# An encoder block on one core: a fifth tile of weight halves, two step orders changed, four stores moved

## The chip, the cores and the metric

The kernel runs on one core of one Trainium2 chip. The metric is device time in microseconds (us), the median of the runs; a lower time is better. One execution was also taken with the hardware profiler, and all rows below come from it.

## What is computed

The reference is one layer of an encoder over 256 tokens of width 2048, in float32:

```python
h = rms_norm(x, g_mix)
qa, ka, va, qb, kb, vb, qc, gt = split(h @ w_in)           # 4096 columns, then 3 x 2048 of gates
oa = dilated_windows(qa, ka, va)                           # 6 heads in 3 groups
ob = grouped_queries(rope(qb), rope(kb), vb)               # 6 heads, 2 of keys
oc = cross_attention(qc, rms_norm(mem, g_mem) @ w_mem_kv)  # 4 heads
merged = sigmoid(gt0)*(oa@w_br_a) + sigmoid(gt1)*(ob@w_br_b) + sigmoid(gt2)*(oc@w_br_c)
x = x + merged @ w_o
hf = rms_norm(x, g_ffn) @ w_ffn_in                         # 2 x 5632 columns
x = x + (silu(hf[:, :5632]) * hf[:, 5632:]) @ w_ffn_out
```

Nearly all of the time goes to the products with the weights, some 273 MB that are read once from HBM.

## The kernel before

**Halves.** A weight tile `raw` is 128 rows by 2 x 512 columns of float32 (512 KB), in one of 6 buffers. It enters TensorE as two tiles in a rounded format: `whi`, the rounded weight (ScalarE, line 358 in `halves`, line 123 in the older `product`), and `wlo`, the rest (VectorE, lines 359 and 124). The activations are held as two halves as well, so each product takes three matmuls. There are 4 buffers each of `whi` and `wlo`.

**Stages.** `beginning` (the memory keys) runs through `run` and `pair`. The qkv blocks and the first gates run through `product`, with the attention as side jobs. Then `heads`, a group of pools for what only attention needs (`s2`, 32 KB a partition), is given up, and `run(everything())` does the rest: `merging` (gates and branches), `projecting` (the product with `w_o`, in two pairs of column blocks, n = 0 and n = 2) and `feeding` (11 pairs of `w_ffn`; after 4, 8 and 11 of them two pairs of `w_ffn_out`).

**Steps.** `pair` computes two column blocks c = 0 and c = 1 for 256 tokens by a list of steps. `d3` and `D3` are the plain product of row tile 3 with block 0 or 1: one `raw`, one pair of halves, 12 matmuls. `f3 g3 h3` with a share of `p` and `q` do the same row tile for both blocks by seven multiplications in place of eight: 21 matmuls for 24, but 3.5 pairs of halves for 2, and four more additions on VectorE (lines 449 to 451 in `g`, 465 in `h`). "Light" below means `d` and `D`; "heavy" means `f g h`. The lists are `STEPS...` in lines 53 to 58. `STEPS_O` serves both pairs of `w_o`, `STEPS_FFN` only the first pair of `w_ffn` (line 828).

**Order.** `run` (line 505) has each step make its halves first (`ready`) and do its matmuls later: `AHEAD` = 3 steps wait in between, so four pairs of halves are in flight. TensorE's instructions and the loads on SyncE's queue stay in the order of the program; the halves of all steps stay in order on ScalarE and on VectorE (`nc.follow`). All the rest is placed by a scheduler at build time, with some at high priority. After each step's matmuls `tick` advances one side job. A job that yields n goes on n ticks later.

**What follows a pair.** When the last step of block c is done, `sums` adds up its banks and `done` uses them. For a pair of `w_o` that is `add`: x is updated (line 779), and two ticks later `transposed` (line 266) turns the new columns, in two halves, into `x1T`, through `tp`, a bank of PSUM that ScalarE and VectorE read in turn, twice each (lines 126 and 127 in `split`). With blocks c = 0 and c = 1 that makes four banks, on four successive ticks: first half of block 0, first half of block 1, second half of block 0, second half of block 1. They stand behind the first four steps of the next pair. Then, after n = 0, `sums_of` builds the `forms`, the sums of tokens that `g`, `p` and `q` of `w_ffn` need.

**Banks.** PSUM's eight banks are two groups of four. The accumulators X, Y and Z of a pair and the first halves of `transposed` share the group `at`; V, Q, W and the second halves share `mm` (lines 272 and 386). Y and V are taken by the first `d`, Z and Q by the first `D`, X by the first `f`, W by the first `g`; they stay taken through the pair.

**Stores.** In the last part of `w_ffn_out` the result is stored by SyncE straight behind its sum (line 847), in the same queue as the loads.

Of the kernel before, what the change touches and what calls it, by code (L numbers as in the profile page):

```python
# [11 lines left out]
F32 = mybir.dt.float32  # L12
F32R = mybir.dt.float32r
# [5 lines left out]
P = 128  # L19
S = 256  # L20
T = S // P
D = 2048
KT = D // P
HD = 128
DFF = 5632
NC = 512
KF = DFF // P
PK = 2
# [23 lines left out]

STEPS = "d0 f1 D0 g1 d4 h1 f2 D4 g2 d5 h2 f3 D5 g3 d6 h3 p0 p2 D6 q0 q2 d7 D7".split()
STEPS_GATE = "d0 D0 d4 D4 f1 d5 g1 D5 h1 f2 g2 d6 h2 f3 g3 h3 p0 p2 D6 q0 q2 d7 D7".split()
STEPS_FFN = "d0 D0 f1 d4 g1 D4 h1 f2 d5 g2 D5 h2 f3 d6 g3 h3 p0 p2 D6 q0 q2 d7 D7".split()
STEPS_O = "d0 D0 d1 D1 f2 d4 g2 D4 h2 d5 f3 D5 g3 d6 h3 p0 D6 q0 d7 D7".split()
STEPS_OUT = "d0 D0 d1 D1 d2 D2 f6 d3 g6 D3 h6 f7 d4 g7 h7 p0 D4 q0 d5 D5".split()
STEPS_OUT2 = "d0 f5 D0 g5 d1 h5 f6 D1 g6 d2 h6 f7 D2 g7 d3 h7 p0 p2 D3 q0 q2 d4 D4".split()
AHEAD = 3


class InOrder:
# [37 lines left out]
def encoder_block(ctx: ExitStack, tc: tile.TileContext, a: dict, out: bass.AP):  # L100
    nc = InOrder(tc)
    const = ctx.enter_context(tc.tile_pool(name="const", bufs=1))
    wp = ctx.enter_context(tc.tile_pool(name="wp", bufs=3))
    big = ctx.enter_context(tc.tile_pool(name="big", bufs=11))
    mid = ctx.enter_context(tc.tile_pool(name="mid", bufs=5))
    small = ctx.enter_context(tc.tile_pool(name="small", bufs=4))
    dram = ctx.enter_context(tc.tile_pool(name="dram", bufs=1, space=bass.MemoryType.DRAM))
    psum = ctx.enter_context(tc.tile_pool(name="psum", bufs=4, space=bass.MemoryType.PSUM))

    def s8(shape, name, dt=F32R, pool=None):  # L110
        return (pool or big).tile(shape, dt, name=name, tag="s8")
# [59 lines left out]
    def start(steps):  # L171

        job = [0, steps]
        side.append(job)
        advance(job)
# [55 lines left out]
    def load_T(src, g, tag):  # L231


        tiles = [s8([P, 4, 2, S], tag) for _ in range(KT // 4)]
        raws, have = {}, set()

        def get(k, fetch=False):
            k0 = k // 2 * 2
            tl = tiles[k // 4]
            if k0 not in raws:  # L240
                raws[k0] = wp.tile([P, 2, S], F32, name="rawT", bufs=2)
                nc.sync.dma_start(out=raws[k0], in_=src[k0 // 2].rearrange("p (k s) -> p k s", s=S))
            if not fetch and k0 not in have:
                have.add(k0)
                for i in range(k0, k0 + 2):
                    split(tl[:, i % 4, 0], tl[:, i % 4, 1], raws[k0][:, i - k0], g[:, i:i + 1])
            return tl[:, k % 4, 0], tl[:, k % 4, 1]
        return get
# [46 lines left out]
    two = const.tile([P, 2], F32, name="two")  # L295
    nc.vector.memset(two[:, :1], 1.0)
    nc.scalar.activation(two[:, 1:], two[:, :1], AF.Copy)
    gh = const.tile([P, 6, HD], F32, name="gh")
    rope = const.tile([P, 2, T, HD // 2], F32, name="rope")
    relb = const.tile([P, A_HEADS], F32, name="relb")  # L300

    def constants():
# [7 lines left out]
    def hold(n, steps):  # L310
        yield n
        yield from steps

    def fetch(get, pace):
        for k in range(0, KT, 2):
            get(k)
            yield pace
# [29 lines left out]
            yield 1  # L347


    def halves(*srcs):  # L350

        hi = wp.tile([P, PK, NC], F32R, name="whi", bufs=4)
        lo = wp.tile([P, PK, NC], F32R, name="wlo", bufs=4)
        n = 0
        for v in srcs:
            v = v.unsqueeze(1) if len(v.shape) == 2 else v
            o = slice(n, n + v.shape[1])
            nc.follow(nc.scalar.activation(hi[:, o], v, AF.Copy))  # L358
            nc.follow(nc.vector.tensor_sub(lo[:, o], v, hi[:, o].bitcast(F32)))  # L359
            n += v.shape[1]  # L360
        return hi, lo
# [140 lines left out]
                    done(c, sums(c))  # L502
            yield ending

    def run(pairs):

        nc.on = True
        waiting = []
        for p in pairs:
            for products in p:  # L510
                waiting.append(products)
                if len(waiting) > AHEAD:
                    waiting.pop(0)()
                    tick()
        for products in waiting:
            products()
            tick()
        nc.on = False

    whole_k = lambda n: [d + str(u) for u in range(n) for d in "dD"]  # L520
    block_pair = lambda w, n: lambda u, c: w[n + c][u]


    headT, V = {}, {}
    heads = ExitStack()
    s2 = heads.enter_context(tc.tile_pool(name="s2", bufs=16))

    def take_slots(ps, slots, r, name="x", eng=nc.gpsimd):
# [140 lines left out]
    def beginning():  # L669
        start(hold(5, row_sums(a["mem"], r_m, 3, "mem")))  # L670
        start(hold(10, constants()))
        start(hold(5, fetch(xT, 1)))
        yield pair(block_pair(a["w_mem"], 0), memT, whole_k(KT // 2),
                   lambda c, r: start(take_slots(r, MEM_SLOTS[4 * c:4 * c + 4], r_m, "mem", nc.vector)), operand=memT)

    run(beginning())
    oT = [s8([P, 4, 2, S], f"oT{i}") for i in range(3)]
    ol = lambda k: (oT[k // 4][:, k % 4, 0], oT[k // 4][:, k % 4, 1])
    for c in range(8):
# [16 lines left out]
    finish()  # L696
    heads.close()
    tail = ctx.enter_context(tc.tile_pool(name="tail", bufs=4))
    mT, x1T, x = [], [], []
    ss1 = const.tile([P, T, 4], F32, name="ss1")  # L700

# [66 lines left out]
    def projecting():  # L768
        x.extend(s8([P, D], f"x{t}", F32) for t in range(T))
        for t in range(T):  # L770
            nc.sync.dma_start(out=x[t], in_=a["x"][t * P:(t + 1) * P, :])
        x1T.extend(s8([P, 2, 4, S], "x1T") for _ in range(4))
        mTl = lambda k: (mT[k // 4][:, 0, k % 4], mT[k // 4][:, 1, k % 4])
        oforms = sums_of(mTl, (2, 3), form_room(2))
        for n in (0, 2):
            def add(c, r, n=n):
                xc = [x[t][:, (n + c) * NC:(n + c + 1) * NC] for t in range(T)]
                for t in range(T):
                    nc.vector.tensor_add(xc[t], r[:, t], xc[t])

                def later():
                    yield 1
                    sq = s4([P, T, NC], "sq")
                    for t in range(T):
                        nc.scalar.activation(sq[:, t], xc[t], AF.Square, accum_out=ss1[:, t, n + c:n + c + 1])
                    yield 2
                    yield from transposed(xc, lambda k, m: (x1T[n + c][:, 0, k], x1T[n + c][:, 1, k]),
                                          lambda k: gT[:, 2, 4 * (n + c) + k:4 * (n + c) + k + 1], 2)
                    if n + c == 1:
                        room.extend(form_room(3))  # L790
                        forms.append(sums_of(x1l, (1, 2, 3), room[:3]))
                    elif n + c == 3:
                        yield 2
                        ssr = small.tile([P, T], F32, name="ss", bufs=1)
                        nc.vector.tensor_reduce(ssr, ss1, axis=AX.X, op=ALU.add)
                        row_scale(ssr, r_f)
                start(urgent(later()))
            yield pair(block_pair(a["w_o"], n), mTl, STEPS_O, add, oforms)


    def feeding():
        for c0, c1 in ((0, 4), (4, 8), (8, KF // 4)):
# [4 lines left out]
            for n in range(c0, c1):  # L807
                halves_of = []

                def hidden(c, v, av=halves_of, late=late if n == c1 - 1 else []):  # L810
# [9 lines left out]
                    def later():  # L820
# [6 lines left out]
                    start(urgent(later()))  # L827
                yield pair(lambda u, c, n=n: a["w_ffn"][n][2 * u + c], x1l, STEPS if n else STEPS_FFN, hidden,
                           lambda u, f: forms[0](u, f))
            pairs = whole_k(2 * (c1 - c0)), whole_k(2 * (c1 - c0))  # L830
            out_forms = None
            if not last:
                pairs = STEPS_OUT, STEPS_OUT2
                sums_of(hTl, (5,), room[3:])
                out_forms = by_pair((5, 6, 7), room[3:] + late)
            for n in (0, 2):
                def output(c, r, n=n, last=last):
                    for t in range(T):
                        rt = r[t] if last else r[:, t]
                        for h in range(2 if last and n + c == 3 else 1):  # L840
                            w = NC if not (last and n + c == 3) else NC // 2
                            o = slice((n + c) * NC + h * w, (n + c) * NC + (h + 1) * w)
                            nc.vector.scalar_tensor_tensor(x[t][:, o], rt[:, h * w:(h + 1) * w],
                                                           r_f[:, 0, t:t + 1], x[t][:, o],
                                                           op0=ALU.mult, op1=ALU.add)
                            if last:
                                nc.sync.dma_start(out=out[t * P:(t + 1) * P, o], in_=x[t][:, o])
                yield pair(lambda u, c, n=n, c0=c0: a["w_ffn_out"][n + c][2 * c0 + u], hTl, pairs[n // 2], output,
                           out_forms)

    def everything():
        for stage in (merging, projecting, feeding):
            yield from stage()

    run(everything())
    finish()


# [82 lines left out]
```

## Time and profile before

| | |
|---|---|
| median of 3 runs | 1421.25 us (1418.86 to 1422.56) |
| the profiled execution | 1424.29 us |
| its span, first to last instruction | 1422.5 us |
| TensorE matmul busy | 1392.6 us (98%) |
| VectorE busy | 1125.9 us (79%) |
| ScalarE busy | 804.5 us (57%) |
| mean granted TensorE clock | 0.996 |

The profiled execution spent 1.8 us outside its span. Busy time of a matmul is drawn longer (0.39 us) than the distance at which matmuls follow each other, so a wait of TensorE has to be read from the starts.

### The profile page before, as it was taken

How to read it: one execution, taken by the hardware profiler on the slowest of the kernel's cores; microseconds unless marked ns; L12 is line 12 of the kernel's file. 1: busy time of each engine (PE TensorE's matmuls, PEld its weight loads, DVE VectorE, ACT ScalarE, POOL GpSimd, SP SyncE). 2: the span in 40 equal slices, each digit the busy share in tenths (PEclk: the TensorE clock that was granted, in tenths of full speed). 3: DMA queues.
4: the chain of work that ended last, by engine and by line, in shares of the span. 5: the costliest groups of instructions: out<-in, count | busy, mean ns of one | idle time of the engine just before them, and what ended most of it. 6: DMA issues, size and time to landing. Idle time of an engine off the chain costs nothing.

```text
span 1422.5 us, 17528 instructions
## 1 busy us (share of the span) xinstructions
PE 1392.6 (98%) x6245; PEld 1136.5 (80%) x6245; DVE 1125.9 (79%) x1481; ACT 804.5 (57%) x1096; POOL 76.7 (5%) x146
## 2 busy tenths in 40 slices
PE   8999999999999999999999999999999999999998
PEld 6778878888878888888778888777888877788886
DVE  5767756755788888879988898988889988898844
ACT  6766545644464564656656556555565664466632
POOL 0024533200000000000000000000000000000000
PEclk9999999999999999999999999999999999999999
DMA  8976535556565665756555666566666656556644
GB/s 296 332 237 206 162 112 185 163 163 188 171 205 180 190 223 175 268 171 186 190 172 193 200 192 197 172 220 190 186 201 196 215 171 203 187 183 202 218 129 162
DMA packets 79416, 277.09 MB, mean 195 GB/s; under 512 B 8992, under 2 KB 11552, under 8 KB 79072
## 3 DMA queue, kind: packets, MB, share of 16 engines
q1 hardware_dynamic: 79184, 275.94, 60.7%
q8 instruction: 49, 0.80, 0.2%
q14 instruction: 39, 0.32, 0.1%
q10 hardware_dynamic: 144, 0.02, 0.0%
HBM read 273.05 MB, written 2.88 MB: 194 GB/s over the span
## 4 chain that ended last, share of the span: by engine, by line
PE 75%; DVE 10%; ACT 5%; issue 5%; DMA 2%; POOL 2%; SPq 0%; ACTq 0%; DVEq 0%; POOLq 0%
PE mm L75 17%; PE mmZ L75 12%; PE mmY L75 11%; PE mmV L75 11%; PE mmQ L75 10%; PE mmX L75 7%; DVE wlo L359 5%; ACT whi L358 4%; PE mmW L75 2%; DMA raw<-in_w_mem 1%; DVE raw L450 1%; PE tp L75 1%; DVE t L449 1%; PE sc L75 1%; POOL rot L579 1%
## 5 line engine op out<-in xcount | busy, mean ns | idle before, releaser
L359 DVE TENSOR_TENSOR wlo<-raw,whi 128x1024 fp32r<-128x1024 f32 (+1 forms) x455 | 518.0, 1153 | 154.1 <-ACT whi L358 149.2
L358 ACT ACTIVATE whi<-raw 128x1024 fp32r<-128x1024 f32 (+1 forms) x455 | 444.7, 1001 | 340.8 <-DVE raw L450 74.5
L75 PE MATMUL mm<-whi,xT 128*128 128x512 f32 x768 | 244.5, 395 | 0.0
L124 DVE TENSOR_TENSOR wlo<-raw,whi 128x1024 fp32r<-128x1024 f32 x100 | 128.7, 1296 | 86.1 <-ACT whi L123 85.6
L75 PEld LDWEIGHTS mm<-whi,xT 128*128 128x128 f32 x768 | 144.4, 189 | 29.7 <-issue 0.8
L123 ACT ACTIVATE whi<-raw 128x1024 fp32r<-128x1024 f32 x100 | 105.7, 1071 | 90.6 <-PE mm L75 83.5
L75 PE MATMUL mm<-wlo,xT 128*128 128x512 f32 x384 | 151.3, 394 | 0.0
L75 PE MATMUL mmY<-whi,x1T 128*128 128x512 f32 x286 | 111.3, 390 | 0.0
L75 PE MATMUL mmV<-whi,x1T 128*128 128x512 f32 x286 | 108.6, 392 | 0.0
L75 PE MATMUL mmZ<-whi,x1T 128*128 128x512 f32 x220 | 85.8, 390 | 0.0
L75 PE MATMUL mmQ<-whi,x1T 128*128 128x512 f32 x220 | 85.7, 389 | 0.0
L75 PEld LDWEIGHTS mm<-wlo,xT 128*128 128x128 f32 x384 | 72.7, 189 | 15.7 <-issue 0.8
L75 PE MATMUL mmX<-whi,forms 128*128 128x512 f32 x236 | 79.7, 390 | 0.0
L359 DVE TENSOR_TENSOR wlo<-t,whi 128x1024 fp32r<-128x1024 f32 x76 | 72.2, 982 | 4.8 <-ACT whi L358 4.6
L358 ACT ACTIVATE whi<-t 128x1024 fp32r<-128x1024 f32 x76 | 63.4, 858 | 1.2 <-PE mmX L75 0.7
L75 PEld LDWEIGHTS mmY<-whi,x1T 128*128 128x128 f32 x286 | 53.7, 188 | 11.4
L75 PEld LDWEIGHTS mmV<-whi,x1T 128*128 128x128 f32 x286 | 53.7, 188 | 11.0
L75 PE MATMUL mmY<-whi,hT 128*128 128x512 f32 x156 | 60.4, 391 | 0.0
L75 PE MATMUL mmV<-whi,hT 128*128 128x512 f32 x156 | 60.1, 392 | 0.0
L75 PE MATMUL mmV<-wlo,x1T 128*128 128x512 f32 x143 | 55.8, 390 | 0.0
L75 PE MATMUL mmY<-wlo,x1T 128*128 128x512 f32 x143 | 55.7, 389 | 0.0
L75 PE MATMUL mmZ<-whi,hT 128*128 128x512 f32 x136 | 53.9, 396 | 1.3 <-ACT whi L358 1.3
(258 smaller groups left out, 2711.5 us busy)
## 6 DMA issues: line engine op xcount, KB each, us to landing
raw<-in_w_ffn SPq DMA_DIRECT2D x176, 512.0 KB, 4.2
raw<-in_w_gate SPq DMA_DIRECT2D x96, 512.0 KB, 4.1
raw<-in_w_ffn_out SPq DMA_DIRECT2D x88, 512.0 KB, 4.3
raw<-in_w_qkv SPq DMA_DIRECT2D x64, 512.0 KB, 4.9
raw<-in_w_o SPq DMA_DIRECT2D x32, 512.0 KB, 4.3
raw<-in_w_br SPq DMA_DIRECT2D x24, 512.0 KB, 3.6
raw<-in_w_mem SPq DMA_DIRECT2D x16, 512.0 KB, 6.3
rawT<-in_memT SPq DMA_DIRECT2D x8, 256.0 KB, 4.3
```

Of the source, the lines that this page charges most:

```text
L75: ins = op(*args, **kw)
L123: nc.scalar.activation(hi, src, AF.Copy)
L124: nc.vector.tensor_sub(lo, src, hi.bitcast(F32))
L358: nc.follow(nc.scalar.activation(hi[:, o], v, AF.Copy))
L359: nc.follow(nc.vector.tensor_sub(lo[:, o], v, hi[:, o].bitcast(F32)))
L449: nc.follow(nc.vector.tensor_add(t3[:, those.index(u)], b2[:, 0], b2[:, 1]))
L450: nc.follow(nc.vector.tensor_add(b2[:, 0], b2[:, 0], b1[:, 0]))
L579: op(ov[:, :, :, c], ov[:, :, :, c], tmp[:, :n])
```

## The change

Four things are done together.

1. `gh`, `rope` and `rawT`, 8 KB a partition, move from pools that live to the end into a pool `early`, which is given up together with `heads`. In the room a pool `more` holds one further pair of `whi` and `wlo`: every fifth call of `halves` takes it. `AHEAD` becomes an argument of `run`: 3 for `beginning`, 4 for `everything`.
2. `STEPS_FFN` has two heavy row tiles, not three, and begins with six light steps.
3. The second pair of `w_o` gets a list of its own, `STEPS_O2`: its heavy steps begin with the second step, and its last six are light.
4. A store becomes a side job: for the pair n = 0 it is put four ticks behind its sum, for n = 2 one tick.

```diff
-STEPS_FFN = "d0 D0 f1 d4 g1 D4 h1 f2 d5 g2 D5 h2 f3 d6 g3 h3 p0 p2 D6 q0 q2 d7 D7".split()
+STEPS_FFN = "d0 D0 d1 D1 d4 D4 f2 d5 g2 D5 h2 f3 d6 g3 h3 p0 D6 q0 d7 D7".split()
 STEPS_O = "d0 D0 d1 D1 f2 d4 g2 D4 h2 d5 f3 D5 g3 d6 h3 p0 D6 q0 d7 D7".split()
+STEPS_O2 = "d0 f2 D0 g2 d1 h2 f3 D1 g3 d4 h3 p0 D4 q0 d5 D5 d6 D6 d7 D7".split()
-AHEAD = 3
...
+    heads = ExitStack()
+    early = heads.enter_context(tc.tile_pool(name="early", bufs=1))
...
-                raws[k0] = wp.tile([P, 2, S], F32, name="rawT", bufs=2)
+                raws[k0] = early.tile([P, 2, S], F32, name="rawT", bufs=2)
...
-    gh = const.tile([P, 6, HD], F32, name="gh")
-    rope = const.tile([P, 2, T, HD // 2], F32, name="rope")
+    gh = early.tile([P, 6, HD], F32, name="gh")
+    rope = early.tile([P, 2, T, HD // 2], F32, name="rope")
...
+    count, more = [0], []
+
     def halves(*srcs):
 
-        hi = wp.tile([P, PK, NC], F32R, name="whi", bufs=4)
-        lo = wp.tile([P, PK, NC], F32R, name="wlo", bufs=4)
+        count[0] += 1
+        pool, n = (more[0], 1) if more and count[0] % 5 == 0 else (wp, 4)
+        hi = pool.tile([P, PK, NC], F32R, name="whi", bufs=n)
+        lo = pool.tile([P, PK, NC], F32R, name="wlo", bufs=n)
...
-    def run(pairs):
+    def run(pairs, ahead):
...
-                if len(waiting) > AHEAD:
+                if len(waiting) > ahead:
...
-    run(beginning())
+    run(beginning(), 3)
...
     heads.close()
     tail = ctx.enter_context(tc.tile_pool(name="tail", bufs=4))
+    more.append(ctx.enter_context(tc.tile_pool(name="more", bufs=1)))
...
-            yield pair(block_pair(a["w_o"], n), mTl, STEPS_O, add, oforms)
+            yield pair(block_pair(a["w_o"], n), mTl, STEPS_O2 if n else STEPS_O, add, oforms)
+
+    def store(t, o):
+        nc.sync.dma_start(out=out[t * P:(t + 1) * P, o], in_=x[t][:, o])
+        yield 1
...
-                                nc.sync.dma_start(out=out[t * P:(t + 1) * P, o], in_=x[t][:, o])
+                                start(hold(1 if n else 4, store(t, o)))
...
-    run(everything())
+    run(everything(), 4)
```

## Rows read from the trace of the kernel before

**Rows 1.** The page, part 1: busy us, share of span, instructions of each engine.

```profile
PE 1392.6 (98%) x6245; PEld 1136.5 (80%) x6245; DVE 1125.9 (79%) x1481; ACT 804.5 (57%) x1096; POOL 76.7 (5%) x146
```

**Rows 2.** Waits of PE, whole span: who waited for whom, us, times, longest.

```profile
PE mmW L75 <- DVE wlo L359: 4.2, 11, 0.8
...
PE mmX L75 <- DVE wlo L359: 2.5, 5, 0.5
...
PE mmW L75 <- ACT whi L358: 0.9, 1, 0.9
```

**Rows 3.** Timeline of PE, one `w_ffn` pair: start, us, engine, line, operation, tiles.

```profile
811.63 0.39 PE L75 MATMUL mmQ<-whi,x1T 128*128 128x512 f32 x1
...
812.31 0.39 PE L75 MATMUL mmW<-whi,forms 128*128 128x512 f32 x1
...
813.39 0.39 PE L75 MATMUL mmZ<-whi,forms 128*128 128x512 f32 x1
```

**Rows 4.** Waits of all engines, whole span, same columns as rows 2.

```profile
DVE wlo L359 <- ACT whi L358: 153.8, 207, 4.1
...
ACT whi L358 <- PE mmV L75: 73.4, 51, 2.9
```

**Rows 5.** Timelines of ACT and of DVE; in brackets the idle time before.

```profile
779.58 1.06 ACT L358 ACTIVATE whi<-raw 128x1024 fp32r<-128x1024 f32 x1 [1.17 <-PE mmQ L75]
...
780.68 2.59 DVE L359 TENSOR_TENSOR wlo<-raw,whi 128x1024 fp32r<-128x1024 f32 x2 [0.72 <-ACT whi L358]
...
929.52 0.68 DVE L449 TENSOR_TENSOR t<-raw 128x512 f32<-128x512 f32 x1
...
939.17 0.68 DVE L449 TENSOR_TENSOR t<-raw 128x512 f32<-128x512 f32 x1
```

**Rows 6.** Timeline of PE, first pair of `w_ffn`.

```profile
700.80 0.60 PE L75 MATMUL tp<-ident,x 128*128 128x128 f32 x4
701.65 0.47 PE L75 MATMUL mmX<-whi,x1T 128*128 128x512 f32 x1 [0.25 <-DVE x1T L127]
...
706.31 0.60 PE L75 MATMUL tp<-ident,x 128*128 128x128 f32 x4
709.48 0.77 PE L75 MATMUL mmW<-whi,forms 128*128 128x512 f32 x1 [2.58 <-DVE x1T L127]
...
712.51 0.39 PE L75 MATMUL mmZ<-wlo,x1T 128*128 128x512 f32 x1
```

**Rows 7.** Stretches: length, busy us of PE, PEld, DVE, ACT, POOL; PE clock; DMA.

```profile
650.40:694.60 44.20, 44.20 (x202) 36.23 (x201) 42.07 (x65) 28.91 (x44) 0.00 (x0) 1.00 0.59 188
...
709.40:712.50 3.10, 3.02 (x7) 2.44 (x8) 1.67 (x9) 0.51 (x2) 0.00 (x0) 0.52 0.38 145
```

**Rows 8.** Timelines of PE and DVE: two transposed banks and their last reads.

```profile
653.19 0.60 PE L75 MATMUL tp<-ident,x 128*128 128x128 f32 x4
653.54 0.48 PE L75 MATMUL mmZ<-whi,mT 128*128 128x512 f32 x1
...
659.47 0.87 DVE L127 SCALAR_TENSOR_TENSOR x1T<-tp,gT,x1T 128x256 fp32r<-128x256 f32 x2
...
697.59 0.60 PE L75 MATMUL tp<-ident,x 128*128 128x128 f32 x4
...
701.03 0.47 DVE L127 SCALAR_TENSOR_TENSOR x1T<-tp,gT,x1T 128x256 fp32r<-128x256 f32 x1
```

**Rows 9.** Waits of SP's queue, whole span, same columns as rows 2.

```profile
SPq L75 <- DVE x L843: 40.4, 9, 19.3
```

**Rows 10.** Timelines of PE and ACT near the end.

```profile
1390.66 0.40 PE L75 MATMUL mmV<-whi,hT 128*128 128x512 f32 x1
...
1391.24 1.06 ACT L358 ACTIVATE whi<-raw 128x1024 fp32r<-128x1024 f32 x1 [4.29 <-DMA raw<-in_w_ffn_out]
...
1393.95 0.40 PE L75 MATMUL mmZ<-whi,hT 128*128 128x512 f32 x1
```

More of the change, by code (lines that the diff above doesn't have):

```diff
@@ L524, in encoder_block @@
     headT, V = {}, {}
-    heads = ExitStack()
     s2 = heads.enter_context(tc.tile_pool(name="s2", bufs=16))
```

## The prediction, made before the result was known

> **What bounds the kernel now.** I read the page first. TensorE is busy 98% of the span, VectorE 79%, ScalarE 57% [rows 1]. So the question is how much of TensorE's time is waiting, and the 98% can't say it, because a matmul is drawn 0.39 us long. From the starts the pace is read: from 811.63 to 812.31 three matmuls pass, 0.227 us each [rows 3]. A listed wait of TensorE is therefore 0.16 us longer than its row says (0.39 - 0.23), and one under some 0.3 us is not listed at all.
>
> The view of TensorE's waits comes next [rows 2]. The first product with forms in a `g` step (mmW) waited 11 times for VectorE's `wlo`: 4.2 + 11 x 0.16 = 6.0 us. The chain X in `p` and `q` waited 5 times: 2.5 + 0.8 = 3.3 us. One mmW waited for `whi`: 1.1 us. Not listed is what rows 3 show: the last `g` of a `w_ffn` pair takes 1.08 us from 812.31 to 813.39 for three matmuls, 0.40 us too long. I find this in 8 of the 11 pairs: 3.2 us. That is 13.6 us of small waits for halves, all in heavy stretches.
>
> Then I asked why the halves come late. VectorE waits 154 us in total for `whi`, and ScalarE's `whi` waits 73 us for a mmV, that is for TensorE to give back a buffer [rows 4]. In a light stretch both are held up by the four tiles: ScalarE idles 1.17 us for mmQ, and VectorE behind it 0.72 us [rows 5]. In a heavy stretch VectorE alone is slow: from one `g` to the next it needs 9.65 us (929.52 to 939.17) [rows 5] for steps whose 39 matmuls take 39 x 0.227 = 8.9 us. So the lead is capped when VectorE has time, and eaten up when it has none.
>
> Two larger waits stand alone. At the start of `w_ffn` mmW begins 3.17 us after the last transposition's start, where such a group otherwise delays its successor by 0.35 us [rows 6, 8]; it waited for a read of `tp`, that is for a bank. Near the end 3.29 us pass from 1390.66 to 1393.95 for three matmuls: 2.6 us too long, behind a load that came late [rows 10].
>
> **The change part by part.**
>
> *Stores.* SyncE's queue stood up to 19.3 us at a store that waited for its sum [rows 9], and the loads behind it came too late: the 2.6 us of rows 10. Now the first store of n = 0 stands behind the load of the sixth of the last pair's 12 steps, the others after later loads. By then their sums are long made, so no load waits. Gain 2.6 us. The stores of the last pair remain behind all loads; nothing waits there, and the price is between 0 and 0.4 us (one more short store issue). I take 0.
>
> *The start of `w_ffn`.* Now W is taken by the fifth step, while V, Q and two second halves of `transposed` hold the four banks of `mm`. Wait: 3.17 - 0.35 = 2.8 us. After it the clock was granted at 0.52, the lower level, 1.2 GHz [rows 7]: the seven matmuls from 709.48 to 712.51 took 3.03 instead of 1.59 us, 1.4 us more [rows 6]. X, the third step, had waited as well: 0.85 - 0.35 = 0.5 us. Together 4.7 us. With the new list X comes seventh and W ninth, some 11 us later than now (four light steps of 12 matmuls), when those banks have been read. One heavy row tile becomes plain: 3 more matmuls, 0.7 us. Net gain 4.0 us. If the cover failed, the 4.7 would stay.
>
> *The fifth tile.* It adds one step of lead. What it can give is bounded above by the 13.6 us of waits, below by 0: where VectorE is the limit, a buffer makes nothing faster. (A loss, a further `wlo` of 1.2 us ahead of a sum, is excluded by the high priority that the sums have.) I price it by the idle time that the four tiles force on VectorE ahead of a heavy stretch, 0.72 us a pair [rows 5]. The 8 waits of 0.40 us are below that and go: 3.2 us. The 17 waits of rows 2, 10.4 us, lie in some ten pairs, often several to a pair; at 0.72 us a pair about 7 us of them go. Sum 10 us, nearer the upper end, since the idle time is there in each pair.
>
> By the Trainium skill, page "Perfetto Trace Analysis", section "Identifying Performance Opportunities", the same gap repeating on the engine that should be saturated can mean that there isn't room enough for the next tile to be allocated. By that rule all 13.6 us would go, and the sum below would be 3.6 us lower. The trace agrees in part: ScalarE does wait for buffers, but in heavy stretches VectorE's 9.65 us stand against 8.9.
>
> *The second pair of `w_o`.* Here the change takes light steps away from the place where it needs them. The four transposed banks of n = 0 fall behind the first four steps, which are now d0, f2, D0, g2. In group `at`, Y, first half 0, X and first half 1 are four; Z, due at D0, is the fifth and must wait until first half 0 has been read. In `mm`, V, Q, second half 0 and W are four; second half 1, behind g2, is the fifth. How long a bank takes to be read is in rows 8: from the end of its transposition at 653.79 to about 659.95, 6.1 us; and from 698.19 to 701.50, 3.3 us. TensorE has less to do meanwhile: f2 and a transposition before Z, 1.36 + 0.35 = 1.7 us; g2 before the other, 1.4 us. Waits: 1.6 to 4.4 us and 1.9 to 4.7 us. VectorE is also short of time there. It was busy 42.1 us in the 44.2 us of this pair [rows 7]; six light halves of 1.2 us now fall at its end, so 35 us of work meet 114 matmuls and four transpositions, 27 us on TensorE. 8 us are missing, less what the lead and the waits for banks cover. I take 6.5 us: about 3 for Z, 2 for the second (VectorE catches up in the first), 1.5 for VectorE; bounds 0 (the scheduler sets the reads first) and 20 (both waits at their longest, VectorE's 8 us on top, the clock falling twice). The Trainium skill, page "Perfetto Trace Analysis", section "Matmuls", asks that accumulation groups rotate through different banks, so that the reading of one overlaps the next one's matmuls; five in a group of four is against it, and no row of before shows it at this place.
>
> *The moved pools.* The same bytes at other places; the tiles of `early` are last used before `merging`, and so nothing waits: 0. Loads are not the limit in the middle, so the raw tiles stay as they are.
>
> **The sum.** -2.6 - 4.0 - 10 + 6.5 = -10.1 us against the profiled 1424.3, that is 1414.2, of which 1.8 lie outside the span. That execution was 3.0 us above the median of 1421.25. Carried over to the median: 1411 us.
>
> **The rivals.**
> (1) The second pair of `w_o` costs nothing: as banks are what TensorE waits for, the scheduler reads them first. For it: reads have high priority, and 3.3 us were reached once. Against it: a bank needs four reads in turn, and 1.7 us are too few for that. Sum -16.6: 1405.
> (2) The fifth tile gives nearly nothing: VectorE in its fixed order sets the pace in heavy stretches. For it: 9.65 against 8.9 us. Against it: the 0.72 us of forced idleness. With 2 us gained the sum is -2.1: 1419. If the tile does not work as a fifth one at all, the result is the same.
> (3) Slower: the start of the second pair of `w_o` breaks up into waits, and the clock goes to its lower level with each. It did so after one wait of 2.58 us. If half of these 27 us run at half speed, that is 13 us, on top of 9 us of waits for banks. Sum -16.6 + 22 = +5.4: 1427. It decides against the change from a loss of 21 us at that place.
>
> **How the numbers follow.** A difference under 0.3%, 4.3 us, is about what a measurement of this kernel can't tell from none: 1417.0 to 1425.5. The forecast of 1411 (1406 to 1416) has 0.55, rival 1 0.15, rival 2 0.22, rival 3 0.08. Rival 2 reaches from 1416 to 1422 and gives 0.04 to faster, the rest to same. Faster 0.74, same 0.18, slower 0.08. The range leaves out rival 3, the lowest part of rival 1 and the highest of rival 2: 1402 to 1421.
>
> **What would show it.** Right: no gap before mmW in the `w_ffn` pairs; the first pair of `w_ffn` without a wait or a fall of the clock; loads evenly spaced through the last `w_ffn_out`; and a wait of TensorE before mmZ and before a `tp` at the start of the second pair of `w_o`, with VectorE's read of `tp` as the releaser, 5 us in all. Wrong: mmW still late for `wlo` in most pairs (rival 2), no wait in the second pair of `w_o` (rival 1), or a stretch there with a clock near 0.5 for more than 3 us (rival 3).

## The result, and the profile after

The changed kernel took 1423.21 us (median of 20 runs, 1420.23 to 1426.12), the kernel before 1420.64 us beside it (20 runs): a ratio of 1.0019, 95% interval 1.0012 to 1.0026. The forecast was 1411, the range 1402 to 1421. The gains came, smaller than forecast, and the second pair of `w_o` took back more than all of them. The profiled execution took 1422.27 us, span 1420.3.

The page, part 1, and the waits of PE, both of the kernel after (columns as in rows 1 and 2):

```profile
PE 1393.0 (98%) x6248; PEld 1138.2 (80%) x6248; DVE 1118.9 (79%) x1474; ACT 796.6 (56%) x1093; POOL 76.5 (5%) x146
```

```profile
PE mmZ L75 <- DVE x1T L129: 3.8, 1, 3.8
PE tp L75 <- DVE x1T L129: 3.0, 1, 3.0
...
PE tp L75 <- DVE x L785: 1.4, 1, 1.4
PE mmW L75 <- DVE wlo L365: 1.2, 3, 0.8
PE mmW L75 <- ACT whi L364: 0.9, 1, 0.9
...
PE mmX L75 <- DVE wlo L365: 0.5, 1, 0.5
```

The page hides the story: TensorE is busy 98% as in rows 1. The list of waits tells it. The small waits of rows 2 went from 10.4 us (0.16 added to each) to 1.2 + 3 x 0.16 for mmW and `wlo`, 0.9 + 0.16 for `whi` and 0.5 + 0.16 for mmX, together 3.4 us. The wait of mmW for `x1T` in rows 6 is gone. In their place stand three new ones, of which two are for banks.

Where the time went is read from the start of TensorE's first matmul in each stage (us; the last line ends at the start of TensorE's last matmul; "before" and "after" are the two profiled executions, the others are experiments told of below, "both in order" the last kernel of "`hT` in order"):

| stage | before | after | old list | list alone | banks apart | both in order |
|---|---|---|---|---|---|---|
| up to `merging` | 377.2 | 374.5 | 375.5 | 376.7 | 376.4 | 375.7 |
| `merging` | 228.9 | 228.1 | 228.2 | 228.8 | 228.2 | 228.2 |
| `w_o`, both pairs | 88.8 | **101.5** | 89.1 | 101.0 | 91.8 | 89.1 |
| first `w_ffn` block | 177.8 | 173.2 | 173.2 | 176.3 | 173.2 | 172.5 |
| its `w_ffn_out` | 87.4 | 85.7 | 85.7 | 87.5 | 85.7 | 85.7 |
| second block | 172.1 | 171.6 | 171.9 | 172.4 | 171.6 | 170.6 |
| its `w_ffn_out` | 87.5 | 85.7 | 85.7 | 87.5 | 85.7 | 85.7 |
| third block (3 pairs) | 129.2 | 128.7 | 128.5 | 129.1 | 128.6 | 127.9 |
| last `w_ffn_out` | 69.2 | 66.7 | 66.7 | 67.4 | 66.7 | 66.7 |

The first line changes by up to 4.1 us between profiled executions that run the same orders there (373.1 in "no transpositions", 377.2 in the kernel before); it is spread, and it is why single profiles are compared stage by stage and medians by their ratios.

Of the 12.7 us in `w_o` nearly every part can be read. Timeline of PE after, the start of the second pair:

```profile
649.95 0.60 PE L75 MATMUL tp<-ident,x 128*128 128x128 f32 x4
...
651.53 0.39 PE L75 MATMUL mmY<-whi,mT 128*128 128x512 f32 x1
651.91 0.33 PE L75 MATMUL tp<-ident,x 128*128 128x128 f32 x1
653.65 0.55 PE L75 MATMUL tp<-ident,x 128*128 128x128 f32 x3 [1.41 <-DVE x L785]
657.97 0.77 PE L75 MATMUL mmZ<-whi,mT 128*128 128x512 f32 x1 [3.78 <-DVE x1T L129]
658.53 0.63 PE L75 MATMUL mmZ<-wlo,mT 128*128 128x512 f32 x1
...
661.90 0.40 PE L75 MATMUL mmQ<-whi,mT 128*128 128x512 f32 x1
...
662.60 0.60 PE L75 MATMUL tp<-ident,x 128*128 128x128 f32 x4
...
664.20 0.40 PE L75 MATMUL mmZ<-whi,forms 128*128 128x512 f32 x1
667.63 0.63 PE L75 MATMUL tp<-ident,x 128*128 128x128 f32 x4 [3.04 <-DVE x1T L129]
668.02 0.48 PE L75 MATMUL mmY<-whi,mT 128*128 128x512 f32 x1
668.33 0.40 PE L75 MATMUL mmY<-wlo,mT 128*128 128x512 f32 x1
668.57 0.55 PE L75 MATMUL mmY<-whi,mT 128*128 128x512 f32 x1
...
672.21 0.62 PE L75 MATMUL mmV<-whi,mT 128*128 128x512 f32 x2
```

Timeline of DVE after (VectorE's reads of the two banks, the last of each last), and windows after with columns as in rows 7:

```profile
654.11 0.48 DVE L129 SCALAR_TENSOR_TENSOR x1T<-tp,gT,x1T 128x256 fp32r<-128x256 f32 x1
...
657.35 0.87 DVE L129 SCALAR_TENSOR_TENSOR x1T<-tp,gT,x1T 128x256 fp32r<-128x256 f32 x2
...
667.01 0.47 DVE L129 SCALAR_TENSOR_TENSOR x1T<-tp,gT,x1T 128x256 fp32r<-128x256 f32 x1
```

```profile
650.40:675.00 24.60, 16.37 (x62) 12.42 (x61) 16.89 (x31) 9.97 (x20) 0.00 (x0) 0.79 0.34 107
649.43:658.23 8.80, 3.61 (x18) 2.46 (x18) 8.34 (x13) 5.56 (x14) 0.00 (x0) 0.82 0.49 144
658.23:664.00 5.77, 5.77 (x21) 4.59 (x21) 0.06 (x1) 1.15 (x2) 0.00 (x0) 0.69 0.14 54
657.90:661.90 4.00, 3.93 (x10) 3.14 (x10) 0.32 (x1) 0.00 (x0) 0.00 (x0) 0.51 0.26 101
668.60:672.20 3.60, 3.60 (x10) 2.83 (x9) 3.60 (x10) 0.18 (x1) 0.00 (x0) 0.53 0.39 117
```

Z begins 6.44 us after the matmul at 651.53, where 0.23 + 0.35 would do: 5.85 us lost. 1.6 of them pass inside the transposition of block 1, which came before VectorE had summed its `x`, and 4.2 go on the bank. Then nine matmuls take 3.93 us (657.97 to 661.90) in place of 2.04 at a granted clock of 0.51: 1.8 us, the 0.09 of the matmul behind a transposition left out. The transposition at 667.63 waits 3.43 - 0.23 = 3.2 us, and nine more matmuls (668.57 to 672.21, clock 0.53) lose 1.6 us. Sum 12.5 us.

The bank that Z waits for was filled at 650.55 (649.95 + 0.60) and read for the last time by 657.83 (657.35 + 0.48, the first of the two reads): a turn of 7.3 us. The second bank was filled at 663.20 and read by 667.48: 4.3 us. VectorE's share says little here: it is busy 16.9 of the 24.6 us, but 8.34 of the 8.80 until the reads that free Z's bank are done, and 0.06 of the next 5.77. The reads stand behind sums and halves in the orders of VectorE and ScalarE (VectorE's first read begins at 654.11, 3.6 us after the bank was filled), and that makes the turn long.

### The profile page after: what moved, and what is told of

It reads as the page before. It is cut to its first block, busy times and chain, and to the rows that moved or that the text cites. A ratio compares the mean times of both kernels' runs of the same rounds, so it can differ in the third digit from the quotient of the medians.

```text
span 1420.3 us, 17529 instructions
## 1 busy us (share of the span) xinstructions
PE 1393.0 (98%) x6248; PEld 1138.2 (80%) x6248; DVE 1118.9 (79%) x1474; ACT 796.6 (56%) x1093; POOL 76.5 (5%) x146
## 4 chain that ended last, share of the span: by engine, by line
PE 79%; DVE 8%; ACT 4%; issue 4%; POOL 2%; DMA 2%; SPq 0%; ACTq 0%; DVEq 0%; POOLq 0%
PE mm L75 15%; PE mmV L75 13%; PE mmY L75 13%; PE mmZ L75 13%; PE mmQ L75 11%; PE mmX L75 8%; DVE wlo L365 3%; ACT whi L364 3%; PE mmW L75 2%; DMA raw<-in_w_mem 1%; PE tp L75 1%; DVE raw L456 1%; DVE wlo L126 1%; POOL rot L584 1%; PE sc L75 1%
## 5 line engine op out<-in xcount | busy, mean ns | idle before, releaser
L126 DVE TENSOR_TENSOR wlo<-raw,whi 128x1024 fp32r<-128x1024 f32 x100 | 128.7, 1296 | 86.0 <-ACT whi L125 85.5
L75 PE MATMUL mmZ<-whi,x1T 128*128 128x512 f32 x224 | 87.5, 391 | 0.0
L75 PE MATMUL mmQ<-whi,x1T 128*128 128x512 f32 x224 | 87.4, 390 | 0.0
```

Source lines behind the costliest of these rows:

```text
L75: ins = op(*args, **kw)
L126: nc.vector.tensor_sub(lo, src, hi.bitcast(F32))
```

## The experiments

Each edit is shown against the kernel named, shortened to the lines that matter. The kernel before was timed anew beside each group (medians 1419.97 to 1420.96).

**Old list.** The changed kernel, both pairs of `w_o` with the list of before.

```diff
-            yield pair(block_pair(a["w_o"], n), mTl, STEPS_O2 if n else STEPS_O, add, oforms)
+            yield pair(block_pair(a["w_o"], n), mTl, STEPS_O, add, oforms)
```

> The changed kernel with STEPS_O for both pairs of w_o, so that only the new list of the second pair is undone. The stage table of the two profiles puts 12.7 us of loss into the w_o stage. Theory A (the loss is the new list's, through the banks and the clock): w_o takes 89 us again, the first w_ffn block stays near 173 us, and the time is 10 us below the kernel before, near 0.993 of it. Theory B (the new list also made the start of w_ffn clean, by its light end): w_o is 89 us, but a wait of 2 to 4 us comes back at the start of w_ffn; 6 to 8 us below the kernel before.

Measured: 1410.97 us, ratio 0.9929 (0.9917 to 0.9941). `w_o` is back at 89.1 us. The other three parts are worth 10 us, and the second list costs 12.2 us (1423.21 - 1410.97).

**List alone.** The kernel before, with the second list and nothing else (four tiles, three steps ahead).

```diff
-            yield pair(block_pair(a["w_o"], n), mTl, STEPS_O, add, oforms)
+            yield pair(block_pair(a["w_o"], n), mTl, STEPS_O2 if n else STEPS_O, add, oforms)
```

> The kernel before with STEPS_O2 for the second pair of w_o and nothing else. Theory A (banks): the waits of TensorE before tp, mmZ and tp and the two falls of the clock appear as in the changed kernel; w_o takes about 101 us, the time is 9 to 13 us above the kernel before (1.006 to 1.009). Theory C (the waits come from the longer lead, which puts more halves ahead of the reads): with three steps ahead they are absent or half as long, and the time is at most 5 us above.

Measured: 1433.29 us, ratio 1.0086 (1.0073 to 1.0100), 12.3 us slower. The waits of PE for banks are the same two, so the loss needs neither the fifth tile nor the fourth step ahead. It does not need the wait for the sum of `x` either, which this kernel does not have:

```profile
PE mmZ L76 <- DVE x1T L128: 4.2, 1, 4.2
PE tp L76 <- DVE x1T L128: 3.7, 1, 3.7
```

**Banks apart.** The changed kernel with the second list kept, but with the transposed banks of the first pair on ticks 3, 4, 7 and 8 in place of 3, 4, 5 and 6. The work is the same. The two transposed banks of a group now stand four ticks apart in place of one, so that more time is left for summing `x` and for reading a bank.

```diff
-                    yield 2
+                    yield 5 if n + c == 1 else 2
                     yield from transposed(xc, ...
-                                          lambda k: gT[...], 2)
+                                          lambda k: gT[...], 2 if n else 1)
```

> The changed kernel with its second list of w_o kept, but the four transposed banks of the first pair further apart: both halves of block 0 on ticks 3 and 4, both of block 1 on ticks 7 and 8, in place of 3, 4, 5 and 6. Theory A (what the second list costs is waits for banks, and the falls of the clock behind them): no wait of Z or tp for x1T, no stretch near 0.5 of the clock between 640 and 680 us, both pairs of w_o 89 to 93 us in place of 101.5, time 1410 to 1415 us. Theory B (VectorE has too little time in a pair that begins heavy, and the banks only show it): the lost time comes back as waits for wlo, w_o stays above 96 us, time above 1417 us.

Measured: 1414.13 us, ratio 0.9952 (0.9940 to 0.9964), 9.1 us better than the change. Waits of PE, and a window with columns as in rows 7:

```profile
PE mmX L75 <- ACT SB L406: 2.1, 1, 2.1
```

```profile
640.00:680.00 40.00, 37.73 (x172) 30.45 (x171) 39.31 (x61) 25.92 (x41) 0.00 (x0) 1.00 0.59 176
```

No wait for `x1T`, no fall of the clock. VectorE now does 39.3 us of work in these 40 us, and TensorE goes on. So banks and the clock behind them were the cause, not the amount of VectorE's work. What is left of the list's price, 2.7 us in `w_o` against the old list, is for the most part a wait that none of the theories had: X, reused as a chain, waits for ScalarE's copy of it (2.1 us). Timeline of ACT at that place:

```profile
676.28 1.06 ACT L364 ACTIVATE whi<-raw 128x1024 fp32r<-128x1024 f32 x1 [1.73 <-PE mmQ L75]
...
677.72 0.59 ACT L406 ACTIVATE SB<-mmX 128x512 f32<-128x512 f32 x1
```

The last matmul into X had started at 673.05. The copy stands in ScalarE's order behind a `whi` that first waits 1.73 us for TensorE to give back a buffer.

**Fifth tile alone.** The change with the lists and the stores of before.

```diff
-STEPS_FFN = "d0 D0 d1 D1 d4 D4 f2 d5 g2 D5 h2 f3 d6 g3 h3 p0 D6 q0 d7 D7".split()
+STEPS_FFN = "d0 D0 f1 d4 g1 D4 h1 f2 d5 g2 D5 h2 f3 d6 g3 h3 p0 p2 D6 q0 q2 d7 D7".split()
-            yield pair(block_pair(a["w_o"], n), mTl, STEPS_O2 if n else STEPS_O, add, oforms)
+            yield pair(block_pair(a["w_o"], n), mTl, STEPS_O, add, oforms)
-                                start(hold(1 if n else 4, store(t, o)))
+                                nc.sync.dma_start(out=out[t * P:(t + 1) * P, o], in_=x[t][:, o])
```

> The kernel before with part 1 alone: room from heads, the fifth pair of halves, four steps ahead. As predicted at first: 10 us below the kernel before. By the stage table (0.7 in merging, 1.7 in each of two w_ffn_out parts, about 0.5 in each w_ffn block): 5 to 6 us below. If the moved pools cost 2 us ahead of merging, which the medians but not the two profiles hint at: 3 to 4 us below.

Measured: 1414.54 us, ratio 0.9950 (0.9937 to 0.9964), 6.4 us by the medians and 7.1 by the ratio. The old list at the start of `w_ffn` still has its wait there, but another one: mmX for VectorE's `rs_v`, 3.0 us.

What the fifth tile does is more than to remove waits. Counted from the starts, a distance between two matmuls over 0.245 us is a wait (less the pace), and the shorter distances tell the pace itself:

| stage (us) | waits with four tiles | waits with five | added by a slower pace | stage shorter by |
|---|---|---|---|---|
| `merging` | 6.4 | 4.3 | 1.4 | 0.7 |
| `w_o`, old list | 0.8 | 0.7 | 0.4 | -0.3 |
| first block, new list | 2.4 | 1.6 | 0.9 | 0.0 |
| each of two `w_ffn_out` | 2.2 | 0.2 | 0.3 | 1.7 |
| second block | 3.5 | 2.0 | 1.0 | 0.5 |
| third block | 2.9 | 1.6 | 0.8 | 0.5 |

("Four" is the kernel before, "five" the kernel after; the first block with four is from "first `w_ffn` list alone" below, `w_o` with five from "old list".) Together, with the digits behind, the waits fall by 9.9 us, and 5.2 us of that go to a slower pace. It is slower at one place: the steps that read the pair in the pool `more`. Timeline of PE after, d7 and D7 of a pair in the second block and the next step's first matmul:

```profile
1043.03 0.39 PE L75 MATMUL mmY<-whi,x1T 128*128 128x512 f32 x1
...
1045.83 0.39 PE L75 MATMUL mmZ<-whi,x1T 128*128 128x512 f32 x1
...
1048.57 0.39 PE L75 MATMUL mmY<-whi,x1T 128*128 128x512 f32 x1
```

The 12 matmuls of this d7 take 2.80 us, 0.233 each, those of D7 2.74. Undisturbed light steps of the second block take 2.79 to 2.80 us in each of the eight profiles with five tiles where the program's count of calls of `halves` is a multiple of five, and 2.72 to 2.76 us elsewhere; with four tiles, in "moved pools alone" too, all take 2.72 to 2.75. Why this pair is slower to read no run shows.

**Stores alone.** The kernel before, with the stores as side jobs.

```diff
-                                nc.sync.dma_start(out=out[t * P:(t + 1) * P, o], in_=x[t][:, o])
+                                start(hold(1 if n else 4, store(t, o)))
```

> The kernel before with the stores as side jobs and nothing else. Theory: the loads of the last w_ffn_out are no longer held behind stores, the 2.6 us of waits at 1390 go, the time is 2.5 us below (0.998), all of it in the last stage. Rival: the loads are late for another reason, such as the transfers of the stores themselves, and the time is the same.

Measured: 1419.89 us, ratio 0.9991 (0.9981 to 1.0001): not told from nothing by itself. The profile shows the step: the last stage took 66.6 us in place of 69.2. But in three other profiles with four tiles and the old stores it took 67.4, 67.9 and 67.9 us. The 2.6 us of rows 10 were an unlucky execution; 0.8 to 1.3 us is what there usually was to gain.

**Moved pools alone**, and **first `w_ffn` list alone**, each on the kernel before.

```diff
-                raws[k0] = wp.tile([P, 2, S], F32, name="rawT", bufs=2)
+                raws[k0] = early.tile([P, 2, S], F32, name="rawT", bufs=2)
-    gh = const.tile([P, 6, HD], F32, name="gh")
+    gh = early.tile([P, 6, HD], F32, name="gh")
-    rope = const.tile([P, 2, T, HD // 2], F32, name="rope")
+    rope = early.tile([P, 2, T, HD // 2], F32, name="rope")
```

> The kernel before with only the moved pools: gh, rope and rawT lie in early, given up with the heads; the four tiles of halves, three steps ahead, the lists and the stores are those of before. Theory A (the place of the bytes costs nothing): within 0.1% of the kernel before, whose median was 1420.96 us when measured beside the first four experiments. Theory B (the moved pools cost something in the first 370 us, where gh, rope and rawT are used; it would account for most of the 2 us by which the stages add up to less than the medians of before and after say): 1422.5 to 1424 us, and the stretch up to the start of merging 1 to 3 us longer than the 377.2 us of before.

```diff
-STEPS_FFN = "d0 D0 f1 d4 g1 D4 h1 f2 d5 g2 D5 h2 f3 d6 g3 h3 p0 p2 D6 q0 q2 d7 D7".split()
+STEPS_FFN = "d0 D0 d1 D1 d4 D4 f2 d5 g2 D5 h2 f3 d6 g3 h3 p0 D6 q0 d7 D7".split()
```

> The kernel before with only the new list of the first pair of w_ffn. Theory A (my term for the start of w_ffn holds by itself, -4.7 of waits and cold clock, +0.7 of matmuls): 1416.5 to 1417.5 us, first w_ffn block 173 to 174 us in place of 177.8, no wait of mmW for x1T and no stretch near 700 to 715 us with a granted clock near 0.5. Theory B (the gain in that stage needs the fifth tile as well, since the fifth tile alone left that block at 177.4 us and the two were only seen together): 1419 to 1421 us, the first block above 176 us, with a new wait for halves in it.

Measured: the pools 1420.46 us, ratio 1.0002 (0.9991 to 1.0012): nothing. The list 1416.53 us, ratio 0.9969 (0.9959 to 0.9980), -4.4 us; the first block takes 173.2 us, and mmW waits no more for `x1T`. It needs no fifth tile.

**No transpositions.** Here the question is why the fifth tile gave 7 us and not 10. In seven pairs of `w_ffn` the last `g` was still late by 0.28 to 0.34 us.

```diff
-yield from transposed([av[:, t] for t in range(T)], ...)
+for h in range(2): split(tl[:, 0, ...], tl[:, 1, ...], av[:, h])   # from SBUF, not from tp
```

> The changed kernel with the old list in both pairs of w_o, and with the transposition of the product in w_ffn left out: hT is split straight from the product in SBUF, so its values are in the wrong order, VectorE and ScalarE do the same number of element operations, and no item of VectorE's order there waits for TensorE's transposition any more. TensorE saves 22 transposed banks of 0.35 us, 7.7 us, in any case, 2.8 us in each block of four pairs. Theory A (the waits of about 0.3 us that stay at the last g of the w_ffn pairs with five tiles are there because VectorE, in its fixed order, stands at items timed by TensorE and loses its lead): these waits go too, the second w_ffn block falls from 171.9 us to below 168.3 us, VectorE's waits at hT vanish. Theory B (VectorE is simply short of time in the heavy stretch): the waits stay or grow, since TensorE now arrives earlier; the second w_ffn block is 169.1 us or more.

Measured: 1395.58 us in a single execution. The second block takes 167.7 us, the last `g` of each pair is on time (the first pair of a block aside), and VectorE's waits at `hT` are gone. A transposed bank cost 0.44 us, not 0.35: the matmul behind it is late too, by 0.09. Three pairs of transpositions, six banks, lie in the block, 2.6 us; the other 1.6 us are waits (counted from the starts, 2.2 us in "old list" and 0.5 here). This speaks for the order, but TensorE's work was changed as well, so it does not settle it.

**`hT` in order**, first VectorE's half alone, then ScalarE's too. This leaves all work in place. `follow` puts an instruction into the fixed order of the halves, here behind the halves of the step four ahead. Against the kernel "old list":

```diff
             nc.scalar.activation(hi, src, AF.Copy)
-            nc.vector.tensor_sub(lo, src, hi.bitcast(F32))
+            nc.follow(nc.vector.tensor_sub(lo, src, hi.bitcast(F32)))       # hT only
```

> The changed kernel with the old list in both pairs of w_o, and one further edit: VectorE's half of hT (the transposed product in w_ffn) is put into the fixed order of the halves, so that it stands behind the halves of the step four ahead and not in front of them; nothing is left out. With the old list alone the kernel took 1411.0 us, VectorE waited 17 times, 8.9 us in all, at hT, and seven last g of w_ffn pairs came 0.17 to 0.24 us late beside the 0.11 us that each of these groups always shows. Theory A (VectorE, coming early to an item that TensorE has not yet delivered, loses there the lead that the fifth tile gave): VectorE's waits at hT fall below 3 us, the late g go, each w_ffn block of four pairs is 0.6 to 1.3 us shorter than 171.9 us, time 1408 to 1410 us. Theory B (VectorE is simply out of time there, and the kernel without transpositions only had less for TensorE to do): the blocks stay within 0.3 us, time 1410.5 to 1412 us.

```diff
-            nc.scalar.activation(hi, src, AF.Copy)
+            nc.follow(nc.scalar.activation(hi, src, AF.Copy))               # hT only
```

> As the kernel with VectorE's half of hT in the fixed order, with ScalarE's half put into that order as well; nothing is left out. With VectorE's half alone the w_ffn blocks became only 0.2 us shorter: the 0.35 us before hT went, but ScalarE still stood at its own half of hT until TensorE had delivered it (0.45 us from 829.22 to 829.67), and VectorE then idled 1.30 us for the whi behind it. Theory A (items timed by TensorE in the fixed order of either engine are what eats the lead): the 1.30 us fall below 0.6 us, the late g shrink again, each w_ffn block of four pairs is 171.1 to 171.5 us. Theory B (VectorE's own chain in the heavy steps, raw in h and then whi and wlo with 0.78 us of idleness three times a pair, is what remains, and hT costs nothing any more): the blocks stay at 171.6 to 171.8 us.

Measured: with VectorE's half 1410.22 us, ratio 0.9930 (0.9917 to 0.9944), and the second block 171.7 us: by its numbers the second theory. With both 1408.16 us, ratio 0.9912 (0.9898 to 0.9927), and the second block 170.6 us: the first, with more than it asked for. The interval overlaps that of "old list" (0.9917 to 0.9941); what tells them apart are the three blocks, 0.7, 1.3 and 0.6 us shorter. The timelines of DVE and ACT at the same place, in "old list", then in "VectorE's half", then in "both":

```profile
830.06 0.69 DVE L365 TENSOR_TENSOR wlo<-raw,whi 128x512 fp32r<-128x512 f32 x1 [0.78 <-ACT whi L364]
831.11 0.69 DVE L126 TENSOR_TENSOR hT<-tp,hT 128x512 fp32r<-128x512 f32 x1 [0.35 <-ACT hT L125]
832.05 1.22 DVE L365 TENSOR_TENSOR wlo<-raw,whi 128x1024 fp32r<-128x1024 f32 x1 [0.25 <-ACT whi L364]
```

```profile
829.25 0.69 DVE L367 TENSOR_TENSOR wlo<-raw,whi 128x512 fp32r<-128x512 f32 x1 [0.78 <-ACT whi L366]
831.24 1.22 DVE L367 TENSOR_TENSOR wlo<-raw,whi 128x1024 fp32r<-128x1024 f32 x1 [1.30 <-ACT whi L366]
...
829.67 0.60 ACT L125 ACTIVATE hT<-tp 128x512 fp32r<-128x512 f32 x1 [0.45 <-PE tp L75]
```

```profile
829.88 0.69 DVE L369 TENSOR_TENSOR wlo<-raw,whi 128x512 fp32r<-128x512 f32 x1 [0.78 <-ACT whi L368]
830.83 1.22 DVE L369 TENSOR_TENSOR wlo<-raw,whi 128x1024 fp32r<-128x1024 f32 x1 [0.26 <-ACT whi L368]
831.97 0.68 DVE L128 TENSOR_TENSOR hT<-tp,hT 128x512 fp32r<-128x512 f32 x1
...
830.70 0.58 ACT L125 ACTIVATE hT<-tp 128x512 fp32r<-128x512 f32 x1
```

First VectorE stands at `hT`. With its half moved it idles 1.30 us at the next `wlo`, because ScalarE still stands at its own `hT` until TensorE has delivered `tp`: the wait was only handed on. With both moved nobody waits for TensorE. What that does to the last `g` is in the timelines of PE, "old list" and then "both":

```profile
848.53 0.39 PE L75 MATMUL mmW<-whi,forms 128*128 128x512 f32 x1
849.00 0.50 PE L75 MATMUL mmW<-wlo,forms 128*128 128x512 f32 x1
...
849.57 0.39 PE L75 MATMUL mmZ<-whi,forms 128*128 128x512 f32 x1
```

```profile
848.36 0.39 PE L75 MATMUL mmW<-whi,forms 128*128 128x512 f32 x1
848.59 0.39 PE L75 MATMUL mmW<-wlo,forms 128*128 128x512 f32 x1
...
849.04 0.39 PE L75 MATMUL mmZ<-whi,forms 128*128 128x512 f32 x1
```

Three matmuls take 1.04 us, then 0.68, which is the pace. The 0.11 us that the expectation called a fixed part of such a group was a wait too.

**The stores once more**, in the kernel with VectorE's half in order.

```diff
-                                start(hold(1 if n else 4, store(t, o)))
+                                nc.sync.dma_start(out=out[t * P:(t + 1) * P, o], in_=x[t][:, o])
```

> As the kernel with hT in order, but with the stores of before, straight behind their sums in the queue of the loads. Theory A (with the fifth tile the stores' move is worth nothing: the last w_ffn_out took 66.7 us with the fifth tile and the old stores, as with both, while without either it took 67.4 to 69.3 us in five profiles): within 0.1% of the kernel with hT in order, last stage 66.6 to 66.9 us. Theory B (the moved stores still matter, and the fifth tile's profile was a lucky one): 1.3 to 2.6 us slower, last stage above 67.4 us.

Measured: 1409.86 us, ratio 0.9930 (0.9918 to 0.9942), last stage 66.7 us. With five tiles the stores' move is worth nothing. (The five profiles without either of which the expectation speaks are four, 67.4 to 69.2 us.) The queue still stands (SP's waits, columns as in rows 9), and ScalarE waits as long for the first late load (ACT, here and then in the kernel before, where it is the one ahead of the load in rows 10). No matmul of the stage is late; the step that needs the load has one more tile of lead:

```profile
SPq L75 <- DVE x L855: 40.9, 9, 19.7
```

```profile
1372.87 1.06 ACT L366 ACTIVATE whi<-raw 128x1024 fp32r<-128x1024 f32 x1 [7.44 <-DMA raw<-in_w_ffn_out]
```

```profile
1385.88 1.06 ACT L358 ACTIVATE whi<-raw 128x1024 fp32r<-128x1024 f32 x1 [7.49 <-DMA raw<-in_w_ffn_out]
```

The best kernel found is thus the change with the old list in `w_o` and `hT` in order on both engines: 1408.16 us, 0.9912 of the kernel before.

## Why the prediction was wrong, step by step

- **Second pair of `w_o`: forecast +6.5, measured +12.2.** Place, cause and order of the two bank waits were right; the size was not. For Z I took 3 us, and it lost 5.85; for the second bank I took 2, and it was 3.2. The banks' turns were 7.3 and 4.3 us, where rows 8 had 6.1 and 3.3: I had counted the reads, and not what VectorE has to do in front of them, the sums of `x` and halves. The 1.5 us that I added for VectorE do not show as a wait of their own; its work is inside the turns. And the clock was left out of the sum. Rows 6 and 7 showed that it falls behind a wait of 2.58 us, and I charged 1.4 us for that when it went away, but charged nothing for two waits that I had just forecast. It cost 1.8 + 1.6 us. That is the largest single error. My bounds, 0 and 20, held the value; by the rows, two reads of 3.3 to 6.1 us (4.7 in the middle) less 1.7 and 1.4 of cover, and 1.4 for the clock on each, give 2 x 4.7 - 3.1 + 2.8 = 9.1 us, the better reading. With the turns and the clock as measured it is 7.3 + 4.3 - 3.1 + 3.4 = 11.9 us.
- **The fifth tile: forecast -10, measured -6.4 to -7.1**, and about 1.3 of that lies in the last `w_ffn_out`, where the forecast had put it under the stores. For the small waits that leaves 5 to 6 us, and the stages agree (4.8). The step that failed is the price of the tile itself. I had set 0 as the lower bound of the gain, called a loss "excluded", and thought of VectorE's order alone; but the matmuls that read the added pair follow each other at 0.233 us and not 0.227, and that takes back 5.2 us. In `merging` 2.1 us of waits gave 0.7. The waits themselves went down by 9.9 us, and that this is so near to 10 is luck: the listed waits of rows 2 fell by 7.0 us, as forecast, but of the 8 unlisted waits of 0.40 us one went, and seven stayed at 0.28 to 0.34 (816.82 to 817.84 for three matmuls): 1.0 us gained, not 3.2. The rest, 1.9 us, came from waits that the rows do not list or draw too short. So "The 8 waits of 0.40 us are below that and go" failed as well. The added lead arises in the light stretch and is lost again before the last `g`, because VectorE and ScalarE, in their fixed orders, stand at `hT`, which TensorE has yet to deliver. Putting `hT` behind the halves gave 0.7 + 1.3 + 0.6 us in the three blocks, 2.7 in all with the digits behind, near to the 2.2 us that those waits still held. So rival 2 named a true mechanism, the fixed order, but at one item only, and VectorE's amount of work does not set the pace there.
- By the page "Perfetto Trace Analysis" of the Trainium skill, section "Identifying Performance Opportunities", repeated gaps can mean missing room. Of the 13.6 us that I had put under it, 8.0 went with room (7.0 listed, 1.0 unlisted), 2.7 went with the order of two instructions, and 2.7 at the start of `merging` stand in both kernels (0.9, 0.8 and 0.5 us, each with its 0.16).
- **Start of `w_ffn`: forecast -4.0, measured -4.4.** Right in its parts: no wait of mmW or X, no fall of the clock.
- **Stores: forecast -2.6, measured -1.3 alone (interval to +0.1) and 0 beside the fifth tile.** The mechanism was right, the size came from one execution, and the sum counted twice a wait that the fifth tile removes too (the last stage takes 66.7 us with the tile and the old stores). **Moved pools: 0**, as forecast.
- **The sum.** The gains were 10.0 us where 16.6 were forecast, and the loss 12.2 where 6.5 was. Rival 3 was the right side: waits, with the clock falling with each. Its point of decision, a loss of 21 us at that place, was tied to gains of 16.6 us; with gains of 10 it decides from 10. I gave it 0.08 because I let its price and the gains vary one at a time.

By the Trainium skill, page "Perfetto Trace Analysis", section "Matmuls", groups should rotate through banks so that the reading of one overlaps the next one's matmuls. The runs agree: the same list with the same banks, four ticks between the two of a group in place of one, loses 9.7 us less in `w_o` (101.5 to 91.8). What a bank's turn has to cover here is four reads in turn with all that stands ahead of them on the engines that read, and not the reads alone.

What stays open: why the matmuls that read the added pair are slower, and about 1 us between the parts measured singly (1.3 + 4.4 + 6.4 to 7.1, less the 1.3 counted twice) and together (10.0), which lies within their intervals.

## What to carry to other kernels

When steps are reordered, count for each rotating buffer what its whole turn takes (producer, transposition, every read, and what the reading engines do ahead of it) against the work of the steps that now lie in that turn, and put the clock's price on each wait that you forecast. When a deeper buffer leaves some waits standing, look in the fixed order of the feeding engines for an item that the bound engine has yet to deliver, and move it on all engines that touch it. Compare the pace of the bound engine before and after as well: an added buffer can have a price of its own. A wait that two edits both remove belongs into the sum once, at the size that several executions show.

## What was not expected of the hardware

Matmuls that read the fifth pair of halves followed each other at 0.233 us, those that read the other four at 0.227 (12 in 2.80 and in 2.72 us). Over the stages from `merging` on that is about 5 us.

The granted clock fell behind TensorE's waits of 2.58 us (rows 6, 7), 3.78 and 3.04 us, to 0.51 to 0.53, the lower level of 1.2 GHz, and lay there for 3.0, 3.9 and 3.6 us. It fell behind the 3.0 us of "fifth tile alone" too (0.58 in the mean from 702.50 to 706.50). In "banks apart" it did not fall behind the wait of 2.12 us, which ended at 678.36 (window, columns as in rows 7):

```profile
678.30:684.00 5.70, 5.64 (x25) 4.63 (x26) 5.04 (x10) 3.22 (x6) 0.00 (x0) 1.00 0.86 313
```

The three longer waits, one of the kernel before and two of the kernel after, cost about one and a half times their length (2.8 + 1.4, 4.2 + 1.8 and 3.2 + 1.6 us), the shorter one only its own.
